# A hybrid diffusion step on one core: the prompt's convolution pool is made 2 KiB smaller, and the long convolution counts 0.55 of its cost when streams take turns

## The chip, the cores and the metric

The kernel runs on one core of a Trainium2 chip. The metric is the device time of one execution in microseconds (us). Engines are called by the profile's names: PE is TensorE (matmuls), PEld its weight loads, DVE is VectorE, ACT is ScalarE, POOL is GpSimd and SP is SyncE, which here issues nearly all DMAs.

## The reference

One trunk layer is computed for 2048 latent tokens and for 256 prompt tokens, D = 1024, in f32. Both groups go through the same head groups:

```
h = rms_norm(x) * (1 + scale1) + shift1;  u = h @ w_in            # 1024 -> 2560 columns
y_pool = pool_mixer(u[:256])          # windows 2/4/8/16 along the sequence, minus the token, 64x64 linear
y_hy   = hyena_mixer(u[256:1024])     # width-3 short convolution, then twice:
         # z = gate_o * (two_sided_fft_conv(z, k_o) + bias_o * z); k_o from a small sine MLP, decayed and normed
y_na   = attend(q, k, v)              # u[1024:2560]; latent: 2-D neighbourhood + 256 cached keys;
                                      # prompt: dense among its 256 tokens
x = x + gate1 * (concat(y_pool, y_hy, y_na) @ w_out)
x = x + gate2 * (relu(rms_norm(x) * (1 + scale2) + shift2 @ w_up)^2 @ w_down)
```

The outputs are both groups' x and the prompt's k and v. The long convolution of the latent tokens has length 2048 (FFT of 4096, done as matmuls with DFT matrices); the prompt's has length 256 (one dense DFT of 512).

## The kernel before, in words

**Three streams.** The program is written as three Python generators that `weave` takes turns among. Each `yield` names a cost. At every turn the stream with the least cost so far, divided by its weight, goes next; a stream that waits for a flag yields None and is passed over. The weights are 2200e3 for `dense`, 850e3 for `latent_mixers` and 700e3 for `prompt_mixers`. The turns fix the order in which instructions are written down. A list scheduler of the tile framework then gives each engine a fixed order at compile time: an instruction that was written earlier goes first when both are ready, and what `latent_mixers` and `prompt_mixers` write counts as 1000 and 2500 instructions earlier than its place. On the chip each engine works through its order and waits on semaphores.

**dense.** For each of five blocks of tokens (four of 512 latent tokens, number 4 is the prompt's 256) it computes the first 1024 columns of u (turns of 10 n each, eight per block, n the block's tokens), then, in the order 3, 4, 0, 1, 2, the q, k and v columns (`qkv_run`; 24 turns of 2600 for a latent block, 12 for the prompt's), then waits for the flag "prompt", then runs the output projection (`head`) and the MLP of the prompt, then of the latent blocks. All its matmuls write the PSUM tile `pm` and are made of three f32r products per f32 product (`mm3`, lines 126 to 128), for which each weight tile `wraw` is split into a high and a low part (ACT line 112, DVE line 115).

**latent_mixers.** It makes the filters of the long convolution (`filters`, with the second filter and the first transform only after the flags "u" and "ln"), then `hyena`: a spectrum product in pool `p2v` (16 steps, turns of 3 x 650), an inverse and forward transform in `p2w` (17 turns of 1300), a second spectrum product in `p2x`, and the last inverse transform in `p2y` (8 turns of 1550). Its matmuls write the PSUM tile `pf`. After the flags "qkv" and "prompt" it runs the latent attention (16 calls of `attend_latent`, each 230 + 8 x 1000 + 4 x 1800).

**prompt_mixers.** After the flags "h2p", "qkv4" (q, k and v of the prompt's block) and "ln" it makes the prompt's filters (pool `pfilt`, its result goes to the DRAM tile `Fpd`), then in pool `phy` the prompt's convolution (`prompt_hyena`, which begins with six `conv3`) and the pooling of both groups (`pooling`), then in pool `pat` the prompt's attention. Then it sets "prompt". Its matmuls write the PSUM tiles `pb` and `pbo`.

**Memory.** Pools without `side` are stacked from the low end of SBUF, those with `side="right"` from the high end. By the tile sizes, per partition: `p2v` and `p2x` hold bytes 107,872 to 161,120 (the last tile, the second `sg` buffer, starts at 159,072); `p2w` and `p2y` end at 159,072; `pfilt` begins at 169,696, `phy` at 159,200 (its first two tiles, `ppl`, lie at 159,200 to 161,248), `pat` at 175,712; all three end at 202,464, where `qkv` begins. A pool may take over bytes of a closed pool; the scheduler then makes its instructions wait for the old pool's.

Of the kernel before, what the change touches and what calls it, by code (L numbers as in the profile page):

```python
# [10 lines left out]
F32 = mybir.dt.float32  # L11
# [8 lines left out]
P = 128  # L20
# [35 lines left out]
def tile_hybrid_step(ctx: ExitStack, tc: tile.TileContext, a: dict):  # L56
# [20 lines left out]
    def pvs(name, i=0, n=1):  # L77
        o = PV[name][0] + i
        return pv[:, o:o + n]
# [26 lines left out]
    def split(pool, raw, shape, tag, lo_eng, bufs=None, n=None, hi_eng=None):  # L106
        hi = pool.tile(shape, F32R, tag=tag + "h", name=tag + "h", bufs=bufs)
        lo = pool.tile(shape, F32R, tag=tag + "l", name=tag + "l", bufs=bufs)
        if n is not None:
            hi, lo = hi[:, :n], lo[:, :n]  # L110
        if hi_eng is None:
            nc.scalar.activation(hi, raw, AF.Copy)  # L112
        else:
            hi_eng.tensor_scalar(out=hi, in0=raw, scalar1=1.0, scalar2=1.0, op0=ALU.mult, op1=ALU.mult)
        lo_eng.tensor_tensor(out=lo, in0=raw, in1=hi.bitcast(F32), op=ALU.subtract)  # L115
        return hi, lo
# [40 lines left out]
    def normed(pool, x, r, g, s, k, bufs, keep=False):  # L157

        n = x.shape[1]
        t = xp.tile([P, 512], F32, tag="raw", name="xn", bufs=3)[:, :n] if keep else x  # L160
        if k % 2:
            hi = pool.tile([P, 512], F32R, tag="hh", name="hh", bufs=bufs)[:, :n]
            lo = pool.tile([P, 512], F32R, tag="hl", name="hl", bufs=bufs)[:, :n]
            nc.vector.scalar_tensor_tensor(out=t, in0=x, scalar=g, in1=r, op0=ALU.mult, op1=ALU.mult)  # L164
            nc.scalar.activation(hi, t, AF.Identity, bias=s)
            nc.vector.scalar_tensor_tensor(out=lo, in0=t, scalar=s, in1=hi.bitcast(F32), op0=ALU.add, op1=ALU.subtract)  # L166
            return hi, lo
        nc.gpsimd.tensor_tensor(out=t, in0=x, in1=r, op=ALU.mult)
        nc.vector.tensor_scalar(out=t, in0=t, scalar1=g, scalar2=s, op0=ALU.mult, op1=ALU.add)  # L169
        return split(pool, t, [P, 512], "h", nc.gpsimd, n=n, bufs=bufs)  # L170

    def weave(*streams):


        live = [[st[0], float(st[1]), 0.0, st[2] if len(st) > 2 else 0] for st in streams]
        while live:
            for s in sorted(live, key=lambda e: e[2] / e[1]):
                try:
                    with tc.high_priority(s[3]) if s[3] else ExitStack():
                        cost = next(s[0])  # L180
                except StopIteration:
                    live.remove(s)
                    break
                if cost is not None:
                    s[2] += cost
                    yield cost
                    break
            else:
                yield None
# [10 lines left out]
    def wait_for(*names):  # L200
        while not done.issuperset(names):
            yield None

    def scope(name, bufs=2, side=None, **kw):
        return tc.tile_pool(name=name, bufs=bufs, side=side, reuse_waits="tile", **kw)
# [355 lines left out]
                fs1d.append((yield from filter_latent(o)))  # L561

    def conv3(hy, j, t0, L):
        u = hy.tile([P, L], F32, tag="cu", name="cu", bufs=2)
        nc.sync.dma_start(out=u, in_=uT[2 + j][:, t0:t0 + L])
        y = hy.tile([P, L], F32, tag="cy", name="cy", bufs=2)
        nc.scalar.activation(y, u, AF.Identity, scale=pvs("cw1", j), bias=pvs("cb", j))
        nc.vector.scalar_tensor_tensor(out=y[:, 1:L], in0=u[:, 0:L - 1], scalar=pvs("cw0", j), in1=y[:, 1:L], op0=ALU.mult, op1=ALU.add)
        nc.vector.scalar_tensor_tensor(out=y[:, 0:L - 1], in0=u[:, 1:L], scalar=pvs("cw2", j), in1=y[:, 0:L - 1], op0=ALU.mult, op1=ALU.add)
        return y  # L570
# [178 lines left out]
    def prompt_hyena(hy, bank):  # L749
        ppl = [[hy.tile([P, 2, P], F32, tag=f"ppl{j}{c}", name="ppl", bufs=1) for c in range(2)] for j in range(3)]  # L750
        for j in range(6):
            comp, half = j // 2, j % 2
            y = conv3(hy, j, NL, NP_)
            tr = bank()
            for e in range(2):
                nc.tensor.transpose(tr[:, e * P:(e + 1) * P], y[:, e * P:(e + 1) * P], ident)
            nc.scalar.activation(ppl[comp][half].rearrange("p e c -> p (e c)"), tr[:, :256], AF.Copy)
            yield 120
# [291 lines left out]
    def latent_mixers():  # L1050
        with scope("aps", 1, space=PSUM) as aps:
            turn = [0]

            def psum(tag=None):
                turn[0] ^= tag is None
                return aps.tile([P, 512], F32, tag=tag or "fz"[turn[0]], name="pf")

            yield from filters(psum)
            done.add("filt")
            yield from wait_for("u")  # L1060
            yield from wait_for("ln")
            with scope("hy") as kp:
                yield from hyena(kp, psum)
            done.add("hyena")
        yield from wait_for("qkv", "prompt")
        with scope("att") as at, scope("attps", 2, space=PSUM) as aps:
            def bank(tag):
                return aps.tile([P, 512], F32, tag=tag, name="p" + tag, bufs={"s": 2, "pt": 2, "o": 1}[tag])

            mask = []  # L1070
            for rc in range(3):
                for cc_ in range(3):
                    nr, ncol = ROWC[rc][1], COLC[cc_][1]
                    m = at.tile([P, nr, ncol], BF16, tag=f"mask{rc}{cc_}", name="mask", bufs=1)
                    nc.gpsimd.dma_start(out=m, in_=a["mask"][rc * 3 + cc_, :, 0:nr * ncol].rearrange("p (r c) -> p r c", c=ncol))
                    mask.append(m)
            for band in range(4):
                yield from wait_for(*(f"qkv{b}" for b in range(max(band - 1, 0), min(band + 2, 4))))
                for hp_ in range(4):
                    yield from attend_latent(at, bank, mask, band, hp_)  # L1080
                done.add(band)
        done.add("att")

    def head(rp, xpool, hpool, bank, which, n, c, src, rows, xs, hT):
# [29 lines left out]
        for k in range(KD):  # L1114
            hT.append(normed(hpool, xs[k], r, G2[:, k, c:c + 1], S2m[:, k, c:c + 1], k, bufs, keep=True))
# [40 lines left out]
    def qkv_run(qp, b, hT=None):  # L1156
        T0, n, c = run_of(b)
        if hT is None:
            r = qp.tile([P, 512], F32, tag="rq", name="rq", bufs=1)[:, :n]
            nc.sync.dma_start(out=r, in_=rsd[:, T0:T0 + n].broadcast_to([P, n]))  # L1160
            hT = []
            for k in range(KD):
                x = xp.tile([P, 512], F32, tag="raw", name="xq", bufs=3)[:, :n]
                nc.sync.dma_start(out=x, in_=xcols("xT_prompt", k, 0, n) if c else xcols("xT_sample", k, T0, n))
                hT.append(normed(hp, x, r, G1[:, k, c:c + 1], S1m[:, k, c:c + 1], k, 9))
        yield from proj_qkv(qp, hT, T0, n)
        done.add(f"qkv{b}")
# [98 lines left out]
    for cost in weave((dense(ctx.enter_context(ExitStack())), 2200e3), (latent_mixers(), 850e3, 1000), (prompt_mixers(), 700e3, 2500)):  # L1266
        assert cost is not None, "streams wait for each other"
# [177 lines left out]
def build(nc, arrays):  # L1445
    a = {}
    for name, v in arrays.items():
        a[name] = nc.dram_tensor(f"in_{name}", v.shape, mybir.dt.from_np(v.dtype), kind="ExternalInput").ap()
    for name, shape in _OUTS:
        a[name] = nc.dram_tensor(f"out_{name}", shape, F32, kind="ExternalOutput").ap()  # L1450
    with tile.TileContext(nc, schedule_with_timeline_sim=True) as tc:
        tile_hybrid_step(tc, a)
# [18 lines left out]
```

## Time and profile before

| | us |
|---|---|
| median of 3 runs (lowest, highest) | 3198.05 (3195.04, 3200.30) |
| the profiled execution, its own time | 3199.58 |
| its span in the profile | 3197.7 |
| PE busy in the span | 3044.0 (95%) |
| DVE, ACT, POOL busy | 1939.3 (61%), 1427.5 (45%), 958.1 (30%) |
| mean granted clock of PE, of full speed | 0.97 |

The span is the time from the first to the last instruction on the core; the profiled execution's own time is 1.9 us longer. Matmuls overlap in the records, so a busy PE need not be at its peak: how many matmuls a stretch holds (the number behind the x) tells more than its busy time.

### The profile page before, as it was taken

The numbers are of one execution on the slowest core, as the hardware profiler recorded it, in microseconds if no ns is written. First come the engines' busy times: TensorE is split into PE (matmuls) and PEld (weight loads), VectorE is DVE, ScalarE is ACT, GpSimd is POOL, SyncE is SP. The second block draws the span as 40 slices with busy tenths as digits, with TensorE's granted clock in tenths as the row PEclk, the third lists the DMA queues.
The fourth block names the chain that finished last, engine by engine and source line by source line (L and its number), as shares of the span: only waits on it lengthen the run. The fifth ranks groups of instructions, "written<-read, shape, count | busy, mean of one in ns | idle before, by whom it ended". The sixth has DMA issues, their size and how long they took to land.

```text
span 3197.7 us, 46181 instructions
## 1 busy us (share of the span) xinstructions
PE 3044.0 (95%) x16901; PEld 2512.5 (79%) x16901; DVE 1939.3 (61%) x3017; ACT 1427.5 (45%) x2721; POOL 958.1 (30%) x832
## 2 busy tenths in 40 slices
PE   5999999899898989999999999899999999999999
PEld 1667788799886879977887778688878888788887
DVE  7677676956777677878766545543564345644443
ACT  3555445545565566656555542332333223332222
POOL 2333233522543333446433321311231111311011
PEclk8999999999997899999999999899999999999999
DMA  6568667746973865553333335233324223332232
GB/s 223 161 211 296 218 208 235 250 149 215 291 240 113 273 194 176 181 183 101 121 118 109 104 110 176 79 93 102 115 92 145 95 97 113 98 119 99 92 99 86
DMA packets 255168, 494.26 MB, mean 155 GB/s; under 512 B 23763, under 2 KB 124824, under 8 KB 254619
## 3 DMA queue, kind: packets, MB, share of 16 engines
q1 hardware_dynamic: 247741, 469.03, 45.2%
q0 software_dynamic: 7200, 22.28, 2.5%
q8 instruction: 134, 2.20, 0.3%
q14 instruction: 93, 0.76, 0.1%
HBM read 421.86 MB, written 70.13 MB: 154 GB/s over the span
## 4 chain that ended last, share of the span: by engine, by line
PE 62%; DVE 2%; DMA 1%; ACT 1%; POOL 1%; issue 1%; SPq 0%; DVEq 0%; ACTq 0%; POOLq 0%
PE pm L126 18%; PE pm L128 18%; PE pm L127 18%; PE po L918 3%; PE ppt L897 2%; PE ps L883 1%; PE ps L884 1%; DVE xn L164 0%; DVE xn L169 0%; DVE wl L115 0%; DMA yraw<-yT 0%; DMA kin<-kT 0%; SPq L1009 0%; POOL ssq L150 0%; PE pm L154 0%
## 5 line engine op out<-in xcount | busy, mean ns | idle before, releaser
L115 DVE TENSOR_TENSOR wl<-wraw,wh 128x1024 fp32r<-128x1024 f32 x460 | 589.5, 1283 | 470.8 <-ACT wh L112 428.8
L112 ACT ACTIVATE wh<-wraw 128x1024 fp32r<-128x1024 f32 x430 | 454.6, 1058 | 781.1 <-PE pm L127 710.4
L126 PE MATMUL pm<-hh,wh 128*128 128x512 f32 (+1 forms) x1920 | 719.8, 377 | 19.6 <-ACT hh L112 11.4
L127 PE MATMUL pm<-hl,wh 128*128 128x512 f32 (+1 forms) x1920 | 718.2, 375 | 3.1 <-DVE hl L166 3.1
L128 PE MATMUL pm<-hh,wl 128*128 128x512 f32 (+1 forms) x1920 | 717.4, 374 | 0.0
L115 POOL TENSOR_TENSOR al<-r,ah 128x512 fp32r<-128x512 f32 (+1 forms) x160 | 199.5, 1248 | 967.0 <-ACT ah L112 966.8
L128 PE MATMUL pm<-ah,wl 128*128 128x512 f32 (+1 forms) x1280 | 475.7, 372 | 0.0
L127 PE MATMUL pm<-al,wh 128*128 128x512 f32 (+1 forms) x1280 | 473.3, 370 | 1.8 <-POOL al L115 1.8
L126 PE MATMUL pm<-ah,wh 128*128 128x512 f32 (+1 forms) x1280 | 473.2, 372 | 0.3 <-ACT wh L112 0.3
L126 PEld LDWEIGHTS pm<-hh,wh 128*128 128x128 f32 x1920 | 366.6, 191 | 101.0 <-issue 13.9
L127 PEld LDWEIGHTS pm<-hl,wh 128*128 128x128 f32 x1920 | 365.7, 190 | 74.5 <-issue 10.0
L128 PEld LDWEIGHTS pm<-hh,wl 128*128 128x128 f32 x1920 | 365.4, 190 | 70.0 <-issue 9.0
L1145 DVE SCALAR_TENSOR_TENSOR x<-pm,gate,x 128x512 f32<-128x512 f32 (+1 forms) x320 | 221.4, 695 | 274.1 <-PE pm L128 273.0
L127 PEld LDWEIGHTS pm<-al,wh 128*128 128x128 f32 x1280 | 240.9, 188 | 44.9 <-POOL al L115 2.0
L128 PEld LDWEIGHTS pm<-ah,wl 128*128 128x128 f32 x1280 | 240.9, 188 | 43.0 <-issue 1.7
L126 PEld LDWEIGHTS pm<-ah,wh 128*128 128x128 f32 x1280 | 240.6, 188 | 42.9 <-DVE x L1145 1.4
L127 PE MATMUL pm<-wl,hh 128*128 128x256 f32 x864 | 249.5, 291 | 5.3 <-DVE wl L115 5.3
L126 PE MATMUL pm<-wh,hh 128*128 128x256 f32 x864 | 247.6, 291 | 5.7 <-ACT hh L112 4.6
L128 PE MATMUL pm<-wh,hl 128*128 128x256 f32 x864 | 247.4, 291 | 3.9 <-POOL hl L115 3.1
L889 POOL TENSOR_SCALAR sS<-sS,rl 128x736 f32<-128x736 f32 (+5 forms) x128 | 126.7, 990 | 218.8 <-DVE rl L888 141.9
L127 PEld LDWEIGHTS pm<-wl,hh 128*128 128x128 f32 x864 | 167.2, 194 | 10.4 <-DVE wl L115 6.6
L126 PEld LDWEIGHTS pm<-wh,hh 128*128 128x128 f32 x864 | 166.5, 194 | 10.9 <-ACT hh L112 7.0
(325 smaller groups left out, 4841.1 us busy)
## 6 DMA issues: line engine op xcount, KB each, us to landing
wraw<-in_w_up SPq DMA_DIRECT2D x160, 512.0 KB
wraw<-in_w_down SPq DMA_DIRECT2D x160, 512.0 KB
wraw<-in_w_qkv SPq DMA_DIRECT2D x60, 512.0 KB
wraw<-in_w_u SPq DMA_DIRECT2D x40, 512.0 KB
dftw<-in_S POOLq DMA_DIRECT2D x40, 512.0 KB, 6.1
wraw<-in_w_out SPq DMA_DIRECT2D x40, 512.0 KB
x<-in_xT_sample SPq DMA_DIRECT2D x64, 256.0 KB
wm<-in_w_mod SPq DMA_DIRECT2D x64, 256.0 KB
```

The costliest lines, as they stand in the source:

```text
L112: nc.scalar.activation(hi, raw, AF.Copy)
L115: lo_eng.tensor_tensor(out=lo, in0=raw, in1=hi.bitcast(F32), op=ALU.subtract)
L126: nc.tensor.matmul(out, lh, rh, start=start, stop=False, **kw)
L127: nc.tensor.matmul(out, lh, rl, start=False, stop=False, **kw)
L128: nc.tensor.matmul(out, ll, rh, start=False, stop=stop, **kw)
L883: nc.tensor.matmul(out, qh[:, qc], krhs, start=True, stop=False, **kw)
L884: nc.tensor.matmul(out, ql[:, qc], krhs, start=False, stop=True, **kw)
L889: nc.gpsimd.tensor_scalar(out=sc_[:, :tot], in0=sc_[:, :tot], scalar1=r, scalar2=1.0, op0=ALU.mult, op1=ALU.mult)
L897: nc.tensor.transpose(tr[:n, q * P:(q + 1) * P], scs[e][:, so:so + n], ident)
L918: nc.tensor.matmul(po[64 * e:64 * e + 64, ocol:ocol + P], vap(e, n), pt[:n, col * P:(col + 1) * P], start=(q == 0), stop=(q == len(chunks) ...
L1145: nc.vector.scalar_tensor_tensor(out=xs[j], in0=po, scalar=gate2[:, j, c:c + 1], in1=xs[j], op0=ALU.mult, op1=ALU.add)
```

## The change

`conv3` gets one buffer instead of two for its input `cu` and for its output `cy` (four tiles of 1 KiB become two), so that `phy` holds 2 KiB less and begins at byte 161,248 instead of 159,200. And `hyena`'s turns are passed through `at_rate`, which multiplies each cost by 0.55 and passes None on, so that `weave` gives it 1/0.55 = 1.8 times as many turns for the same progress of the other streams. No instruction is added or removed; the order of all of them may move.

```diff
+    def at_rate(stream, f):
+
+        for cost in stream:
+            yield cost and cost * f
...
     def conv3(hy, j, t0, L):
-        u = hy.tile([P, L], F32, tag="cu", name="cu", bufs=2)
+        u = hy.tile([P, L], F32, tag="cu", name="cu", bufs=1)
         nc.sync.dma_start(out=u, in_=uT[2 + j][:, t0:t0 + L])
-        y = hy.tile([P, L], F32, tag="cy", name="cy", bufs=2)
+        y = hy.tile([P, L], F32, tag="cy", name="cy", bufs=1)
...
             with scope("hy") as kp:
-                yield from hyena(kp, psum)
+                yield from at_rate(hyena(kp, psum), 0.55)
             done.add("hyena")
```

## Rows read from the trace of the kernel before

**Rows 1.** The page, part 2: PE busy and granted clock, 40 slices of 80 us.
```profile
PE   5999999899898989999999999899999999999999
PEclk8999999999997899999999999899999999999999
```

**Rows 2.** Stages: PE, PEld, DVE, ACT, POOL busy (x instructions), PEclk, DMA share, GB/s.
```profile
526.00:640.00 114.00, 96.11 (x659) 84.12 (x659) 99.20 (x136) 59.92 (x114) 67.54 (x50) 0.91 0.79 256
640.00:764.00 124.00, 117.62 (x964) 115.46 (x964) 68.23 (x92) 51.97 (x98) 25.42 (x23) 1.00 0.46 145
764.00:893.00 129.00, 119.00 (x868) 113.91 (x867) 93.87 (x143) 70.84 (x145) 69.14 (x89) 0.96 0.91 296
893.00:947.00 54.00, 50.73 (x396) 48.74 (x395) 46.07 (x62) 34.43 (x71) 22.72 (x17) 0.97 0.76 238
947.00:1020.00 73.00, 55.76 (x259) 42.11 (x258) 54.53 (x88) 43.27 (x97) 35.98 (x29) 0.75 0.39 119
1020.00:1106.00 86.00, 77.07 (x560) 72.99 (x559) 64.14 (x88) 47.51 (x79) 23.82 (x28) 0.87 0.74 239
1106.00:1140.00 34.00, 22.70 (x173) 21.83 (x173) 19.36 (x31) 15.79 (x29) 13.18 (x17) 0.85 0.96 281
```

**Rows 3.** The same stages, instructions on `pm` alone: PE, PEld, DVE, ACT.
```profile
947.00:1020.00 73.00, 0.32 (x3) 0.12 (x1) 0.00 (x0) 0.00 (x0) 0.75 0.39 119
1020.00:1106.00 86.00, 51.72 (x396) 49.57 (x397) 11.36 (x24) 2.71 (x7) 0.87 0.74 239
1106.00:1140.00 34.00, 20.82 (x163) 20.33 (x163) 2.21 (x5) 1.49 (x4) 0.85 0.96 281
```

**Rows 4.** The tiles' first and last starts: prompt filters, conv3, spectrum, prompt attention.
```profile
L747 SPq DMA_DIRECT2D Fpd<-Fp x2: 326/367/408, 448.7 to 492.8; - x2
...
L565 SPq DMA_DIRECT2D cu<-uT x6: 319/420/667, 767.9 to 785.7; - x6
...
L661 ACT ACTIVATE sg<-pf x9: 577/581/602, 601.6 to 766.3; 128x512 f32<-128x512 f32 x9
...
L953 PE MATMUL pb<-ident,sS x32: 272/421/476, 934.7 to 1019.9; 128*128 128x128 f32 x32
```

**Rows 5.** Stages, instructions on `pf` alone.
```profile
526.00:640.00 114.00, 37.40 (x222) 32.07 (x222) 33.79 (x50) 14.20 (x24) 0.91 0.79 256
640.00:764.00 124.00, 9.54 (x60) 7.91 (x60) 10.59 (x16) 4.15 (x7) 1.00 0.46 145
...
947.00:1020.00 73.00, 36.61 (x180) 30.44 (x181) 28.37 (x42) 12.52 (x21) 0.75 0.39 119
1020.00:1106.00 86.00, 29.20 (x158) 24.78 (x158) 10.15 (x15) 10.88 (x20) 0.87 0.74 239
```

**Rows 6.** The stage 947 to 1020, instructions on `pb` alone.
```profile
947.00:1020.00 73.00, 12.82 (x52) 8.84 (x52) 4.15 (x6) 10.71 (x34) 0.75 0.39 119
```

**Rows 7.** The same stage, instructions on `pbo` alone.
```profile
947.00:1020.00 73.00, 9.83 (x24) 3.40 (x24) 0.00 (x0) 1.14 (x3) 0.75 0.39 119
```

**Rows 8.** What PE waited for from 1020 to 1140: total us, times, longest.
```profile
PE ps L883 <- ACT qh L991: 9.1, 1, 9.1
PE pf L126 <- ACT vsh L112: 3.1, 1, 3.1
PE pf L127 <- DVE vsl L115: 2.5, 2, 1.6
...
PE pf L703 <- DVE z L678: 1.7, 2, 0.9
```

**Rows 9.** DVE groups by shape, 526 to 640: busy, mean ns.
```profile
L115 DVE TENSOR_TENSOR ysl<-Y,ysh 128x512 fp32r<-128x512 f32 x12 | 10.5, 876 | 0.7 <-ACT ysh L112 0.6
...
L647 DVE TENSOR_TENSOR Y<-pf,F 64x512 f32<-64x512 f32 x13 | 8.8, 676 | 0.6 <-ACT F L641 0.5
```

**Rows 10.** A DVE group from 640 to 800.
```profile
L115 DVE TENSOR_TENSOR ysl<-Y,ysh 128x512 fp32r<-128x512 f32 x4 | 2.7, 685 | 0.3 <-ACT ysh L112 0.3
```

**Rows 11.** Latent attention: the first and last load, the first and last transpose.
```profile
L969 SPq DMA_DIRECT2D kin<-kT x16: 326/355/584, 1117.2 to 1732.0; - x16
...
L897 PE MATMUL ppt<-ident,sS x672: 270/273/421, 1142.4 to 1895.4; 128*128 128x128 f32 x96, 128*120 128x128 f32 x48, 128*96 128x128 f32 x8, 128*24 128x128 f32 x8
```

## The prediction

> **What bounds the kernel now.** I read the page's slices first: PE is the engine that is nearly always busy, and the reader is to see the thin spots, slices 12 to 14, where the granted clock also dips to 0.7 [rows 1]. The first slice and the single dips after slice 24 are a start and block changes that the diff does not touch. Then I cut the middle into stages by what each stream was doing [rows 2]. From 640 to 764 us PE took 964 matmuls in 124 us, one per 0.1286 us: that is dense work with little beside it, the full rate. From 764 to 893, with prompt work and the long convolution beside dense, it is one per 0.1486 us; from 526 to 640 one per 0.173. From 947 to 1020 only 259 matmuls ran in 73 us, with the granted clock at 0.75: part of that stage ran at 1.2 instead of 2.4 GHz, behind idle time on PE. By tile the reader sees why: in those 73 us dense started 3 matmuls, after which it started 396 in the next 86 [rows 3]. Dense had finished qkv and stood at "prompt", whose attention made its last transposes at 1019.9 [rows 4]; what ran was the second spectrum and the prompt's attention [rows 5 to 7]. So the stage is bounded by the prompt stream's end, and around it PE is starved.
>
> Why is the prompt that late? Its filters were stored at 492.8, its convolution's first load was issued at 767.9, and between them lies the end of the first spectrum, whose last `sg` was made at 766.3 [rows 4]. By the tile sizes `phy` takes bytes that `p2v`'s last `sg` buffer held (159,200 against 161,120), so I read these 275 us as a wait for memory. The spectrum itself was held back: 222 `pf` matmuls from 526 to 640, then 60 in the next 124 us [rows 5], while PE was full of dense work that had been written earlier.
>
> **The change, part by part.** Costs of turns: the u columns are 4 x 40960 + 20480 = 184,320; blocks 3 and 4 of qkv are 62,400 and 31,200. So dense stands at 277,920 / 2200e3 = 0.1263 when "qkv4" is set. The filters cost 70,800, so hyena begins at 70,800 / 850e3 = 0.0833 and has by then (0.1263 - 0.0833) x 850e3 = 36,600: before, `p2v` (31,200) was closed and `p2w` open, so `phy` could lie on `p2v`'s bytes. With 0.55 it has 66,500 real units, past `p2v` and `p2w` (53,300): `p2x` is open and ends at 161,120, and only the smaller `phy`, from 161,248, fits beside it. The two edits therefore go together.
>
> *conv3 with one buffer.* Nothing is computed less. The prompt's convolution no longer waits for `p2v`; what it still waits for is older (the second filter's transforms and the prompt's own filters, which end between 490 and 520). Its 256 us from 764 to 1020 [rows 2] then lie at some 520 to 780, or 60 us later if crowded; dense needs "prompt" at about 1008, so over 150 us of slack hide it. The price of one buffer: each of six loads waits on SP for the conv before it, and weight loads stand behind it on that queue. All six went out in 18 us [rows 4], some 3 us each. Bounds: nothing, as three `wraw` buffers and the slack cover it, and 18 us if each of six waits held a weight load that PE needed. I take nothing.
>
> *at_rate.* Hyena's 96,900 units count 53,300, so it is written out when dense stands at (70,800 + 53,300) / 850e3 = 0.146 instead of 0.197: 0.7 into the third qkv block instead of half into the fifth. The holding from 640 ends: 60 matmuls at the pace of 222 in 114 us need 31 of those 124 us, so 93 us are saved and hyena's chain, 526 to 1106, would end at about 1013. That is where qkv ends, as follows.
>
> *The sum.* Moved ahead of qkv's end: 180 + 158 `pf`, 52 `pb`, 24 `pbo`, together 414 matmuls [rows 5 to 7]. Their price is not shown; bounds 0.1286 (53 us) and 0.173 (72 us) each. I take 0.1486, the stage most like it (61.5 us): qkv ends at 947 + 61.5 = 1008.5. Then come the 396 + 163 `pm` matmuls that stood done at 1140 [rows 3]: 559 x 0.1286 = 71.9 us. From 1020 to 1140 there were 733 matmuls, 94.3 us of work in 120, so 25.7 us of pauses; 7.3 of them PE spent on hyena's `vsh`, `vsl` and `z` [rows 8], which are past. The others stay, 18.4 us: the norm inside the prompt's head, and the first attention matmul, for which PE stood 9.1 us. The state of 1140 is reached at 1008.5 + 71.9 + 18.4 = 1099, 41 us earlier. After that PE is full in nearly every slice [rows 1], so the gain is kept: 3199.6 (the profiled execution) - 41 = 3158.5. The median lies 1.5 below that execution: 3157.
>
> With the bounds: at 53 us and pauses cut to the 9.1, 947 + 53 + 72 + 9 = 1081, 59 us earlier (3139). At 72 us and all 25.7, 1117: 23 earlier (3175). The 18 us of conv3 on top would leave 5.
>
> **A row that speaks against it.** The work moves into stages where DVE is already 99.2 busy of 114 us [rows 2]. There the f32r split `ysl`, with both inputs in SBUF, took 876 ns [rows 9]; from 640 on, with POOL a third as busy, 685 [rows 10]. The product that reads one input from PSUM took 676 beside the same POOL work [rows 9]. The prompt's pooling brings more POOL work beside the spectrum, and so longer DVE instructions. The Trainium skill (SBUF — State Buffer, Who interferes with whom) says the same as a rule: DVE and GpSimd share a port pair under an exclusive lock, and a DVE instruction with two SBUF inputs waits a GpSimd one out. By that rule the crowded stretch would be paced by DVE and the time would be the third rival's; the trace agrees that such instructions stretch, and no run here shows yet whether PE then starves.
>
> **The rivals.**
>
> *More than forecast.* The pauses go too, and attention, which then starts with the prompt's head instead of 50 us into its MLP, fills its norm: the 59 us of the lower bounds, the last 9.1, and up to 12 of the 18 us in which PE stood from 526 to 640 [rows 2], if prompt work fills them: 59 to 80 us, 3130. For it: the prompt's head had no partner but hyena's last transforms. Against it: PE stood for attention's start itself [rows 8].
>
> *Attention's catch-up takes half.* When "qkv" is set, latent stands at 0.146 and dense at 0.2114, so (0.2114 - 0.146) x 850e3 / 15,430 = 3.6 attention calls are written before dense's next turn, against 0.8 before. A call took (1895.4 - 1117.2) / 16 = 48.6 us beside dense [rows 11]. If 2.8 calls run at double pace, 68 us, and PE has only 259/73 of 964/124 (0.46) to do, as from 947 to 1020, 37 us go; if dense fills in, nothing. The middle, 18: 3176. Against it: the list order lets ready dense matmuls through.
>
> *DVE paces the crowded stretch (slower).* DVE's work from 526 to 947 is 307 us, 54.5 come in from 947 to 1020 [rows 2], and some 35 of the next stage's 64 (an estimate by its 158 `pf` matmuls): 397 us in 482.5, 0.82 full. It was 0.87 full at most by stage, but 0.73 from 764 to 893, when the prompt ran [rows 2]. If dependences and POOL hold DVE to a fill f, qkv ends at 526 + 397 / f, and it decides against the change below 0.756, where that passes 1051 and the 41 us are gone. At 0.72 it ends at 1077: 27 us later than before, 3225.
>
> *It does not do what it says.* If another thing held the prompt (SP's order, PSUM banks), or the order puts it behind hyena, dense still stands at "prompt" near 1020: hyena merely leaves the stage 947 to 1020 emptier. 3198. Against it: filters and convolution stood 275 us apart with every input there.
>
> **How the numbers follow.** Forecast 0.54 (its own range 3139 to 3178), more 0.13, catch-up 0.13, no effect 0.09, DVE 0.11. The time is the likeliest case's, 3157. The range goes from 3118 (80 us, the upper end of the second case) to 3197: it leaves out the DVE case and part of the no-effect case. A measurement of this kernel tells 0.2%, 6.4 us, from no change. Faster: 0.54 + 0.13 + 0.13 = 0.80; same 0.09; slower 0.11.
>
> **What would show it.** Right: `cu` loads near 520; the prompt's last transposes before 850; no hold of `pf` from 640 to 764; dense's first `w_out` matmuls right behind its last qkv ones, at 1000 to 1015, and no stage of 70 us with 259 matmuls. Attention's first `kin` load then stands near 1015 instead of 1117.2. Wrong: qkv's end past 1040 with DVE over 0.8 busy all the way (third rival); `pm` matmuls thin after attention's start (catch-up); `cu` still behind `sg` (no effect). The likeliest error is the price of the 414 moved matmuls.

## The result: 32 us faster, and the profile after

| | before | after |
|---|---|---|
| median of 4 runs each, side by side (lowest, highest), us | 3196.55 (3192.04, 3200.30) | 3165.04 (3163.24, 3167.24) |
| ratio, 95% interval | | 0.9896 (0.9881, 0.9911) |
| span of the profiled execution, us | 3197.7 | 3161.5 |
| PE not busy in the span, us | 153.7 | 138.9 |
| mean granted clock | 0.970 | 0.978 |

The forecast was 3157, the time is 3165: the medians lie 31.5 us apart, where 41 was forecast, and the interval of the ratio is clear of 1. The thin slices 12 to 14 of [rows 1], counted from 0, have filled. Part 2 of the page after, PE busy and granted clock in 40 slices of 79 us:

```profile
PE   5999998889998999999999999899999999999999
PEclk8999999999999999999999999999999999999999
```

The reader sees what was bought and what was paid: slices 12 to 14, 8-9-8 with the clock at 7-8-9 before, are at 8-9-9 with the clock at 9, while slices 6 to 8, 9-8-9 before, are now at 8. The stages show the same. First PE, PEld, DVE, ACT, POOL (busy, instructions), granted clock, DMA share and GB/s, to be laid beside [rows 2]; then the instructions on `pf` alone, beside [rows 5]:

```profile
526.00:640.00 114.00, 94.26 (x567) 78.09 (x567) 105.57 (x154) 62.27 (x135) 83.99 (x83) 0.88 0.85 282
640.00:764.00 124.00, 113.01 (x849) 105.87 (x849) 95.37 (x143) 66.45 (x145) 50.22 (x45) 0.97 0.51 161
764.00:893.00 129.00, 119.87 (x937) 113.66 (x937) 68.97 (x93) 64.09 (x123) 37.32 (x40) 0.99 0.80 263
893.00:980.00 87.00, 84.78 (x700) 84.37 (x699) 72.42 (x101) 54.60 (x106) 38.33 (x29) 0.98 0.63 196
980.00:1060.00 80.00, 69.45 (x505) 65.73 (x504) 72.56 (x99) 47.05 (x82) 33.68 (x34) 0.87 0.66 226
1060.00:1094.00 34.00, 34.00 (x291) 34.00 (x290) 23.31 (x31) 21.00 (x33) 8.28 (x12) 1.00 0.89 284
1094.00:1140.00 46.00, 38.44 (x297) 37.16 (x296) 31.09 (x58) 24.48 (x49) 12.76 (x16) 0.89 0.83 266
```

```profile
526.00:640.00 114.00, 26.87 (x150) 22.20 (x151) 25.12 (x37) 9.45 (x16) 0.88 0.85 282
640.00:764.00 124.00, 21.11 (x126) 18.02 (x126) 16.51 (x25) 8.34 (x14) 0.97 0.51 161
764.00:893.00 129.00, 31.82 (x216) 27.88 (x216) 8.24 (x12) 10.73 (x18) 0.99 0.80 263
893.00:980.00 87.00, 25.35 (x174) 22.53 (x174) 27.94 (x41) 11.28 (x19) 0.98 0.63 196
```

Up to 764 us PE started 567 + 849 = 1416 matmuls against 659 + 964 = 1623 before, at a lower clock and with DVE 93% busy in the first stage. From 764 on it is fuller, and the stage of 73 us with 259 matmuls is gone. Hyena's own matmuls in the first stage fell (222 to 150): the prompt's work came between them.

The streams by tile, to be laid beside [rows 4] and [rows 11] (times of the first and last start at the end): the prompt's filters, its `conv3`, the 16 `sg` of the first spectrum, hyena's first transform load behind that spectrum, the prompt's last attention transposes, the latent attention's loads and transposes.

```profile
L752 SPq DMA_DIRECT2D Fpd<-Fp x2: 327/368/408, 445.4 to 489.5; - x2
...
L570 SPq DMA_DIRECT2D cu<-uT x6: 319/330/583, 520.0 to 564.5; - x6
...
L666 ACT ACTIVATE sg<-pf x16: 579/598/602, 558.4 to 776.5; 128x512 f32<-128x512 f32 x16
...
L673 SPq DMA_DIRECT2D V<-d1d x16: 360/377/623, 779.3 to 1070.7; - x16
...
L958 PE MATMUL pb<-ident,sS x32: 270/272/327, 709.4 to 809.2; 128*128 128x128 f32 x32
...
L974 SPq DMA_DIRECT2D kin<-kT x16: 319/336/471, 1107.7 to 1729.6; - x16
...
L902 PE MATMUL ppt<-ident,sS x672: 270/272/476, 1131.1 to 1880.8; 128*128 128x128 f32 x96, 128*120 128x128 f32 x48, 128*96 128x128 f32 x8, 128*24 128x128 f32 x8
```

The prompt is the part that moved: `cu` 248 us earlier, its last transposes 211 earlier. Hyena hardly did: the first spectrum's last `sg` is 10 us *later*, the latent attention's first transposes 11 earlier.

Dense itself tells where the gain stands. All kernels start 12,271 `pm` matmuls, and dense's parts end at the same numbers in the kernels before and after (within a part the order differs); counted in the records, the start of the n-th:

| dense matmul no. | what it is | before | after | change |
|---|---|---|---|---|
| 3657 | the last of qkv | 947.0 | 980.3 | +33 |
| 4214 | the state of 1140 us in the forecast | 1139.9 | 1093.8 | -46 |
| 5288 | about 1357 before | 1356.8 | 1308.9 | -48 |
| 7056 | attention is over | 1969.4 | 1933.7 | -36 |
| 12271 | the last | 3193.4 | 3157.1 | -36 |

Dense's place is not the whole state of PE, so the -46 and -48 flatter the change. At no. 4214 attention's start, which costs a pause, lies behind the kernel before and still ahead of the kernel after; and at no. 5288 the kernel after had started 154 attention matmuls fewer (`ps`, `ppt` and `po` by their records). The -36 behind attention is the gain.

What PE waited for from 1020 to 1140, the two longest, beside [rows 8]:

```profile
PE pm L126 <- ACT r L1132: 7.2, 1, 7.2
PE pf L127 <- DVE ysl L115: 3.0, 2, 2.2
```

The 9.1 us for attention's start did not go: they became the 7.2. The `r` of line 1132 is not the norm but the relu in the prompt's MLP (the norm's is line 135), and what ACT did just before it shows why it was late:

```profile
1111.80 2.41 ACT L877 ACTIVATE kst<-kin 64x704 fp32r<-64x704 f32 x3 [4.07 <-DMA kin<-kT]
1114.12 1.71 ACT L877 ACTIVATE ckst<-cin 64x256 fp32r<-64x256 f32 x4
1115.86 0.39 ACT L1132 ACTIVATE r<-pm 128x256 f32<-128x256 f32 x1
```

ACT works in its fixed order. Attention's first keys (`kst`, `ckst`) stood in it ahead of the relu; ACT waited 4.1 us for their load and worked 4.1 on them, and dense, which needs the relu, waited 7.2. In the kernel before, PE stood at attention's own first matmul for the same load.

### The profile page after: what moved, and what is told of

It is laid out like the page before. It is cut to its first block, busy times and chain, and to the rows that moved or that the text cites. A ratio compares the mean times of both kernels' runs of the same rounds, so it can differ in the third digit from the quotient of the medians.

```text
span 3161.5 us, 46164 instructions
## 1 busy us (share of the span) xinstructions
PE 3022.6 (96%) x16901; PEld 2494.6 (79%) x16901; DVE 1936.3 (61%) x3017; ACT 1428.6 (45%) x2721; POOL 951.3 (30%) x832
## 4 chain that ended last, share of the span: by engine, by line
PE 81%; DVE 8%; DMA 5%; issue 3%; ACT 2%; POOL 1%; SPq 1%; DVEq 0%; ACTq 0%; POOLq 0%
PE pm L126 22%; PE pm L127 22%; PE pm L128 22%; PE po L923 3%; PE ppt L902 2%; PE ps L888 1%; DVE wl L115 1%; PE ps L889 1%; PE pf L516 1%; PE pf L127 1%; DMA xq<-in_xT_sample 1%; PE pf L126 1%; PE pf L128 1%; PE pf L435 1%; DMA dftw<-in_S 1%
## 5 line engine op out<-in xcount | busy, mean ns | idle before, releaser
L126 PE MATMUL pm<-hh,wh 128*128 128x512 f32 (+1 forms) x1920 | 719.3, 377 | 22.7 <-ACT hh L112 12.8
```

The costliest lines, as they stand in the source:

```text
L126: nc.tensor.matmul(out, lh, rh, start=start, stop=False, **kw)
```

## The experiments

Twelve kernels ran. One table first, so that each group below can refer to it. "Prompt" is the start of the last `pb<-ident,sS` transpose, "spectrum" that of the first `V` load (the first spectrum is over), "hyena" that of the last `pf` matmul, "attention" that of the first `ppt` transpose. "Lost" is worked out from the view by stages, as the sum over nine stages from 526 to 2040 us (cut at 640, 764, 893, 985, 1092, 1200, 1330, 1480) of PE's not-busy time plus (1 - granted clock) x width, and given for 526 to 764 / 764 to 1200 / 1200 to 2040. For the stage 947 to 1020 of [rows 2], for instance, it is 17.2 + 18.3 = 35.5 of 73 us.

| kernel | time | ratio (95%) | prompt | spectrum | hyena | attention | lost |
|---|---|---|---|---|---|---|---|
| before | | 1 | 1019.9 | 778.0 | 1104.8 | 1142.4 | 35/93/40 |
| after | 3165.0 | 0.9896 (0.9881, 0.9911) | 809.2 | 779.3 | 1091.0 | 1131.1 | 48/49/28 |
| e1 pool alone | 3199.0 | 1.0002 (0.9993, 1.0012) | 811.6 | 837.4 | 1158.9 | 1200.1 | 51/68/44 |
| e2 0.70 alone | 3186.4 | 0.9961 (0.9946, 0.9975) | 993.1 | 747.9 | 1091.5 | 1132.2 | 38/76/38 |
| e3 both, 0.70 | 3190.1 | 0.9976 (0.9967, 0.9986) | 808.0 | 795.8 | 1114.6 | 1150.8 | 50/59/33 |
| e6 both, 0.60 | 3183.4 | 0.9943 (0.9922, 0.9963) | 810.1 | 792.1 | 1104.7 | 1147.5 | 49/62/32 |
| e5 both, 0.50 | 3169.6 | 0.9905 (0.9884, 0.9927) | 814.1 | 783.5 | 1100.5 | 1141.0 | 47/54/27 |
| e4 both, 0.40 | 3196.3 | 0.9995 (0.9985, 1.0005) | 810.4 | 763.2 | 1092.6 | 1136.0 | 52/73/40 |
| e7 pooling last | 3192.0 | 0.9974 (0.9964, 0.9984) | 753.7 | 772.9 | 1118.3 | 1157.2 | 47/68/31 |
| e8 latent lead 3000 | 3184.1 | 0.9947 (0.9928, 0.9967) | 813.2 | 707.3 | 1038.2 | 1074.4 | 58/63/37 |
| e9 0.55, first spectrum | 3165.1 | 0.9887 (0.9868, 0.9905) | 815.4 | 786.0 | 1101.4 | 1142.5 | 48/55/28 |
| e10 0.55, after it | 3207.7 | 1.0024 (1.0013, 1.0035) | 808.5 | 836.3 | 1159.2 | 1202.5 | 54/70/44 |
| e11 prompt lead 1500 | 3187.9 | 0.9956 (0.9941, 0.9971) | 813.3 | 706.0 | 1040.4 | 1076.9 | 58/67/33 |
| e12 pool, latent lead 1800 | 3186.8 | 0.9952 (0.9934, 0.997) | 815.7 | 712.4 | 1060.0 | 1094.5 | 60/65/33 |

The differences of the sums of "lost" to the kernel before go with those of the spans within 15 us (before to after: -42, the span -36), so to that accuracy the time of every kernel is PE's pauses and the slow clock around them. The times of events are those of one profiled execution, which can lie some us from the median (e9's took 3172.2, its median is 3165.1).

### The parts, each alone (e1, e2), and both at 0.70 (e3)

`e1_pool_only`: the smaller pool, no factor. `e2_rate_only_070`: the old pool with 0.70; by the tile sizes `phy` with two buffers (43,264 bytes) doesn't fit above `p2x` (41,344 left), so 0.55 alone was not tried. `e3_both_070`: both at 0.70.

```diff
-                yield from at_rate(hyena(kp, psum), 0.55)
+                yield from hyena(kp, psum)                   # e1
+                yield from at_rate(hyena(kp, psum), 0.70)    # e2 (cu, cy with bufs=2) and e3
```

> conv3 with one buffer, hyena at its full cost. Theory A, the gain comes from the prompt's stream ending before qkv does, wherever hyena stands: conv3's loads near 520 us, no stage in which dense waits for the prompt, and 0.985 to 0.993 of the kernel before, like the full change. Theory B, the share of hyena carries at least half: the long convolution is held behind dense and its end, with the start of the latent attention, moves past 1130 us (1106 and 1117 before), and the time is 0.994 to 1.0.

> conv3 with two buffers (phy lies on p2v's bytes), hyena's cost times 0.70, the least factor near 0.55 at which p2x is not yet open when phy is placed. Theory A: phy still waits for the first spectrum, so the prompt ends late and dense waits; hyena's spectrum is held less, so phy starts some 60 to 100 us earlier than 768 and part of the gain comes through that: 0.994 to 0.999. Theory B: 0.990 to 0.994, as most of the full change.

> Both parts, factor 0.70 instead of 0.55. Theory A: within 0.003 of the full change (0.987 to 0.993). Theory B: between the full change and the pool's part alone, nearer to the kernel before by a third of the share's part.

The pool alone frees the prompt (811.6) and gains nothing: theory A, by which the prompt's early end is the gain wherever hyena stands, falls in e1. B, by which hyena's share carries at least half, is right there, but not in size elsewhere: e2 came out at 0.9961, in A's range and above B's, and e3 at 0.9976, where B has some 0.993. The two effects don't add either: at 0.70 the pool's part is nothing that these intervals can tell (e2, e3). Where e1's gain goes is seen in dense: it ends qkv at 971.3, passes no. 4214 at 1098.4 and no. 5288 at 1303.1 (54 us ahead of before, more than after, but with the least attention work done), and no. 7056 at 1970.7, level with before. Stages of e1, all instructions, then `pm` alone:

```profile
1357.00:1391.00 34.00, 29.32 (x174) 20.64 (x173) 22.15 (x67) 22.44 (x69) 16.02 (x16) 0.76 0.40 114
...
1423.00:1441.00 18.00, 13.29 (x91) 9.49 (x91) 16.44 (x32) 12.82 (x33) 12.73 (x12) 0.86 0.37 104
```

```profile
1357.00:1391.00 34.00, 2.51 (x7) 1.26 (x5) 0.00 (x0) 0.00 (x0) 0.76 0.40 114
...
1423.00:1441.00 18.00, 2.08 (x4) 1.33 (x5) 0.00 (x0) 0.71 (x2) 0.86 0.37 104
```

Dense starts 7 matmuls in 34 us: it has done the prompt's head and MLP and stands at the head of the first latent block, which needs attention's output. It waited 31.2 us before no. 5475, and the load `yraw<-yT` of that output had gone out only at 1382.9. The 4 in 18 us are the norm inside that head, where the kernel after stands as well (16.8 us between two `pm` matmuls here, 14.9 there). Attention began 69 us later than in the kernel after, because hyena did: its first spectrum ended at 837.4 instead of 778.0. The same stage of the kernel after, `pm` alone:

```profile
1357.00:1391.00 34.00, 22.63 (x91) 16.31 (x90) 5.68 (x8) 0.00 (x0) 1.00 0.40 121
```

So the wait at "prompt" turned into a wait for the first latent block's attention, as long as hyena is late. e2 is the mirror: hyena's end is that of the kernel after, but the prompt is at 993.1, dense stands at "prompt" for 61 us, and about a third of the gain is there:

```profile
943.00:1004.00 61.00, 0.71 (x6) 0.52 (x6) 0.82 (x2) 0.00 (x0) 0.85 0.48 151
```

### Other factors (e4, e5, e6)

```diff
-                yield from at_rate(hyena(kp, psum), 0.55)
+                yield from at_rate(hyena(kp, psum), 0.40)    # e4; 0.50 in e5, 0.60 in e6
```

> Both parts, factor 0.40: hyena is written out earlier still, the second spectrum before the prompt's filters. Theory A, and hyena paced by the prompt's work and by DVE rather than by its place in the order: hyena ends within 15 us of the full change's 1092 and the time is within 0.003 of it. Theory B: hyena ends 30 us or more earlier, attention starts as much earlier, and the time is 0.983 to 0.988.

> Both parts, factor 0.50. The factors 1.0, 0.70, 0.55 and 0.40 gave 1.0002, 0.9976, 0.9896 and 0.9995. Theory C, smooth: the best factor lies near 0.5 between two costs (hyena late makes attention late; hyena early starves dense), so 0.50 gives 0.988 to 0.993. Theory D, each factor is another draw of the fixed order, whose stalls fall where they fall: anything from 0.988 to 1.0, with hyena's end within 20 us of 1092 all the same.

> Both parts, factor 0.60. Theory C: 0.990 to 0.994, between 0.55 and 0.70. Theory D: anything from 0.988 to 1.0; what tells is PE's idle time plus half its time at the low clock, which should account for the difference to the kernel before within 5 us in either case.

From 1.0 to 0.40 the ratios are 1.0002, 0.9976, 0.9943, 0.9896, 0.9905, 0.9995: a valley with its floor at 0.50 to 0.55, which speaks for theory C: the gain isn't one lucky order, as 0.50 has it too. But the valley is narrow, six points fit D's range as well, and D is not excluded. (e6's pauses and clock fell some 6 us more than its span, about the 5 expected of either theory.) Neither theory of e4 came out: hyena ended where A has it, but the time is not after's, and B's earlier end and gain are missing. At 0.40 the spectrum ended 16 us earlier than after, dense's qkv 23 later (1003.8), and hyena no earlier (1092.6): dense paid and nothing came back. Why hyena's later part then took 329 us instead of 312 was not found. Nor is it shown why the valley is so steep: e3's attention starts 8 us after e9's below (1150.8 against 1142.5), and its time is 25 us longer.

### Is it the crowd on DVE and POOL? (e7)

The pooling of both groups is taken out of the turns with the prompt's convolution and put behind the prompt's attention, in a pool of its own.

```diff
-                yield from weave((prompt_hyena(fp, bank), 14000), (pooling(fp, bank), 8100))
+                yield from prompt_hyena(fp, bank)
...
+            with scope("ppool", side="right") as fp:
+                yield from pooling(fp, bank)
```

> Both parts, factor 0.55, and the pooling (whose window sums run on GpSimd) behind the prompt's attention in a pool of its own instead of beside the prompt's convolution. Theory E, the first spectrum is paced by VectorE and GpSimd in the crowded stretch from 526 to 650: its f32r split falls from 1.1 us toward 0.88, qkv's end and hyena's end move 15 us or more earlier (987 and 1092 with the full change), time 0.982 to 0.987. Rival: the fixed order of PE holds hyena (46 us from 686 to 732 with the full change), hyena's end stays within 10 us of 1092 and the time within 0.003 of the full change's 0.9896.

DVE's splits with two SBUF inputs had indeed grown, from 876 ns [rows 9] to 1173 from 526 to 640, with POOL busy 84 of 114 us. The kernel after:

```profile
L115 DVE TENSOR_TENSOR ysl<-Y,ysh 128x512 fp32r<-128x512 f32 x8 | 9.4, 1173 | 0.7 <-ACT ysh L112 0.7
...
L652 DVE TENSOR_TENSOR Y<-pf,F 64x512 f32<-64x512 f32 x9 | 6.1, 676 | 0.5 <-ACT F L646 0.5
```

The product with a PSUM input stayed at 676. That agrees with the rule that the prediction cited (the Trainium skill, SBUF — State Buffer, Who interferes with whom). In e7 POOL falls to 49.7 us there and the split to 847 ns; two views of e7, the stage and the group:

```profile
526.00:640.00 114.00, 98.22 (x622) 84.05 (x621) 97.23 (x156) 56.74 (x114) 49.72 (x36) 0.90 0.83 271
```

```profile
L115 DVE TENSOR_TENSOR ysl<-Y,ysh 128x512 fp32r<-128x512 f32 x9 | 7.6, 847 | 2.0 <-ACT ysh L112 2.0
```

But what is lost up to 764 us is the same 47 against 48, the spectrum ends only 6 us earlier, and the time is 0.9974. So theory E falls as far as POOL goes: the longer DVE instructions are there, but with the split back at the length it had before (876) the spectrum is hardly earlier, and there is more loss from 764 to 1200 (68 against 49). DVE itself stayed 97.2 of 114 us busy, so whether its own work paces the spectrum is not decided. The rival missed too: the hold stayed, but hyena ended 27 us later (1118.3) and the time is 0.008 above after's. Why was not found.

### Which half of hyena needs the share (e9, e10)

`at_rate` gets bounds in cost units; the first spectrum is the first 31,200 of hyena's 96,900.

```diff
-    def at_rate(stream, f):
+    def at_rate(stream, f, lo, hi):
...
+        done = 0
         for cost in stream:
-            yield cost and cost * f
+            yield cost and cost * (f if lo <= done < hi else 1.0)
+            done += cost or 0
...
+                yield from at_rate(hyena(kp, psum), 0.55, 0, 31200)      # e9
+                yield from at_rate(hyena(kp, psum), 0.55, 31200, 1e9)    # e10
```

> The convolution pool is the smaller one, and the factor 0.55 holds only for the first spectrum's steps (31,200 of the long convolution's 96,900 cost units); from its transforms on each turn counts in full. So the whole stands for an even factor of (0.55 x 31,200 + 65,700) / 96,900 = 0.86. Theory F: only where the long convolution's end is written relative to dense counts, so the time lies on the line between the even factors 1.0 (1.0002 of the time before) and 0.70 (0.9976): 0.9985 to 0.9995. Theory G: the hold of the first spectrum behind dense work is what costs, so this half has at least half of the gain of the whole change: 0.991 to 0.995.

> The reverse: the first spectrum's turns count in full, the factor 0.55 holds from its transforms on (65,700 units). The whole stands for an even factor of (31,200 + 0.55 x 65,700) / 96,900 = 0.69. Theory F (the place of the written end): as the even factor 0.70, 0.996 to 0.998. Theory G (the first spectrum's hold): little of the gain is left, 0.998 to 1.001. If the crowd around the first spectrum were what the change loses, this would beat it: below 0.988, with the long convolution's end before 1090 us.

This is the clearest pair. The share on the first spectrum alone gives the whole gain (0.9887, with after's 0.9896 inside its interval); on the two thirds behind it, it gives nothing (1.0024, and the same late spectrum as e1). So theory F, by which only the written end counts, is wrong, and G holds, more strongly than it was put: the whole gain instead of half, and e10 a little above its range. e9 also sets the early prompt apart from hyena: its attention starts when that of the kernel before did (1142.5 against 1142.4), its prompt ends 204 us earlier, and the whole gain is there. First `V` loads of e9, then of e10:

```profile
L675 SPq DMA_DIRECT2D V<-d1d x16: 359/377/1050, 786.0 to 1081.1; - x16
```

```profile
L675 SPq DMA_DIRECT2D V<-d1d x16: 370/374/643, 836.3 to 1139.6; - x16
```

From its first `V` load to its last matmul hyena takes 312 to 348 us in all fourteen kernels, whatever its turns count there (e1 322, after 312, e10 323): that part isn't set by the share. What the share moves is the end of the first spectrum, which the early prompt had pushed from 778 to 837 and 0.55 pulls back to 779.

### Earlier still, by another way (e8, e11, e12)

`e8_latent_lead_3000`: the change, and what the latent stream writes counts as 3000 instead of 1000 instructions earlier. `e11_prompt_lead_1500`: the change, with the prompt's lead 1500 instead of 2500. `e12_pool_and_latent_lead_1800`: the pool, no factor, latent lead 1800.

```diff
-    ... (latent_mixers(), 850e3, 1000), (prompt_mixers(), 700e3, 2500)):
+    ... (latent_mixers(), 850e3, 3000), (prompt_mixers(), 700e3, 2500)):    # e8; 1800 in e12
+    ... (latent_mixers(), 850e3, 1000), (prompt_mixers(), 700e3, 1500)):    # e11
```

> Both parts, factor 0.55, and what the latent stream writes counts as 3000 instructions earlier than its place instead of 1000. If PE's holding of hyena comes from dense's place in the list, the hold from 686 to 732 goes, hyena ends 30 us or more before 1092 and attention starts as much earlier; time 0.980 to 0.988 if dense is not starved by it, 0.990 to 1.0 if it is. If the hold comes from when the scheduler thought hyena's inputs would be ready, nothing of hyena moves by more than 15 us.

> The whole change (0.55, smaller pool), but what the prompt's stream writes counts as 1500 instead of 2500 instructions earlier. In the changed kernel the prompt ended at 814 us and dense asked for it at about 985, 170 us later. Theory H: the prompt takes turns from the long convolution there that it doesn't need; with a smaller lead the prompt ends at 830 to 950 us, the long convolution 10 to 25 us before 1091, and the time is 0.983 to 0.988 of the time before. Theory I: the gain is a balance of all three streams, in which the long convolution's place counts against dense and the prompt's slack is filled work anyway: 0.989 to 0.996, and the long convolution's end stays within 8 us of 1091.

> The smaller pool, no factor on the long convolution, but what the latent stream writes counts as 1800 instead of 1000 instructions earlier. With the pool alone the time was that of before (1.0002): the wait went from the prompt's end to the first attention work, which began at 1187 us. Theory F': it is the latent stream's place in the list against dense that the factor sets, so a lead can replace it: the attention's first matmul before 1150 us and 0.990 to 0.996. Rival: the share in the turns does something that a lead doesn't (it moves the turns of the other two streams too): 0.998 to 1.002.

All three pull the spectrum's end to 706 to 712 us and attention's start to 1074 to 1095, and all three lie at 0.995. The hold of the spectrum thus comes from its place in the list: with enough lead it goes (from 686 to 732 us 52 `pf` matmuls in e8, 6 in the kernel after). A lead can stand for the share in part (F' in e12), but more of it isn't better. In e11 both theories missed: hyena came 51 us earlier, not 10 to 25 (H) or none (I), the prompt's end stayed at 813, and the time was in I's range for another reason. A stage of e11, all instructions, then `pm` alone, and the same of the kernel after:

```profile
1012.00:1078.00 66.00, 37.70 (x248) 34.17 (x247) 37.11 (x64) 29.11 (x54) 21.57 (x29) 0.74 0.80 254
```

```profile
1012.00:1078.00 66.00, 23.08 (x162) 21.27 (x161) 7.58 (x16) 0.84 (x2) 0.74 0.80 254
```

```profile
1012.00:1078.00 66.00, 59.81 (x454) 57.20 (x453) 55.80 (x75) 41.81 (x70) 23.33 (x28) 0.90 0.78 274
```

By the way of counting above, e11 loses 45.5 us in this stage and the kernel after 12.8; the difference is as large as that of their whole sums (158.5 against 125.2). One wait makes most of it. PE's longest from 1012 to 1085, and what ACT and POOL did before it ended:

```profile
PE pm L154 <- POOL ssq L150: 19.6, 1, 19.6
```

```profile
1061.67 2.42 ACT L877 ACTIVATE kst<-kin 64x704 fp32r<-64x704 f32 x3 [9.24 <-DMA kin<-kT]
1063.99 1.72 ACT L877 ACTIVATE ckst<-cin 64x256 fp32r<-64x256 f32 x4
1065.73 0.42 ACT L149 ACTIVATE sqr<-x 128x256 f32<-128x256 f32 x1
```

```profile
1065.65 0.89 POOL L1025 TENSOR_TENSOR Tt<-bias,mask 128x264 f32<-128x264 f32 x1 [9.63 <-DMA bias<-in_biasw]
1066.50 0.90 POOL L150 TENSOR_TENSOR ssq<-ssq,sqr 128x256 f32<-128x256 f32 x1
```

It is attention's start again. Its first keys and bias stand in the orders of ACT and POOL ahead of the last square (`sqr`) and sum (`ssq`) of the norm in the prompt's head. Both engines wait some 9 us for attention's loads, dense waits for the norm, hyena has ended, and no other matmul runs. e8 has the same wait with 19.1 us; in the other twelve kernels PE's longest wait within some 10 us of attention's first `kst` is 4.8 to 11.1 us. So what stands behind attention's first loads in the fixed orders decides what its start costs. e12 doesn't have the long wait (8.7 us), and its time of 0.995 is not accounted for by it.

## Why the prediction was right, and where its steps were not

- **The wait at "prompt" is a wait for memory**: right. `cu` went out at 520, the prompt's transposes ended at 809, and the pool alone (e1) does that.
- **Price of one buffer for `conv3`**: the six loads took 44.5 us instead of 18, 26 more, and as dense asked for "prompt" only at 980, it cost nothing.
- **at_rate ends the hold, and hyena ends at 1013**: wrong; this is the step that failed. The spectrum was crowded by the prompt (150 `pf` matmuls instead of 222 up to 640) and still held after (126 up to 764); it ended at 779, where it was before, and hyena at 1091; the sign that went with it, attention's first `kin` load near 1015, came at 1107.7. The prediction took the two edits as two gains. The runs showed that the first edit costs the first spectrum 59 us (837.4 against 778.0) and the second gives 58 back.
- **414 matmuls move ahead of qkv's end for 61.5 us**: too many, too cheap. By the stages 3053 were started from 526 to 980, against 2887 from 526 to 947 [rows 2]: 166, of which 108 are `pf`, for 33 us, 0.20 us each and above the upper bound of 0.173. The term came out at +33 where +61.5 was forecast.
- **From qkv's end to the state of 1140 us**: forecast 71.9 + 18.4 = 90.3 us, measured 980.3 to 1093.8, 113.5, since 230 `pf` matmuls that were taken as past still ran there. The state came at 1093.8 instead of 1099, but without attention's start, whose 9.1 us the forecast had put into the 18.4 and which came right behind (7.2 us, and 10.2 us at half the clock from 1111.4, another 5.1). With it the state is at about 1106, 34 us earlier instead of 41.
- **The total**: 41 us forecast, some 34 measured at that state, out of two terms that were far off: qkv ended 28 us sooner than forecast, and what follows took some 35 us longer. That the errors oppose each other has a reason, since hyena's work that didn't move ahead of qkv's end had to be done behind it; that they cancel to 7 us is luck.
- **The gain is kept**: right. 36 us are left at the end, and from 1200 to 2040 us the kernel after lost 28 us against 40. The second rival, attention's catch-up (18 us given back while attention runs), has no sign here.
- **DVE paces the crowded stretch**: DVE was busy 342.3 of 454 us from 526 to 980 (the first four stages), a fill of 0.754, at the value (0.756) where this rival was to decide. It didn't decide, since DVE's work in the stretch was 342 us, not 397: hyena had moved less. From 526 to 764 the loss rose from 35 to 48 us; that DVE's crowd is the cause is not shown (e7).
- **No effect, or the whole of the pauses**: the first is ruled out for the whole change, but it is what the pool alone gives (1.0002), by another mechanism than the one named: not that the prompt stays late, but that hyena becomes late. Of the second, attention's start kept its pause, 7.2 us instead of 9.1.

What is shown: the early prompt isn't enough (e1, e10), and the share is needed only in the first spectrum (e9). That the early prompt is needed for the whole gain rests on e2 and e9: hyena as early as after without it gives 0.9961, attention as late as before with it 0.9887. It is not shown at one factor, since 0.55 doesn't fit without the smaller pool and at 0.70 the pool adds nothing. What is open: why the gain falls off so steeply on both sides of 0.50 to 0.55, why 0.40 and e7 slow hyena's later part, and where e12 loses what its lead should have gained.

## What to carry to other kernels

When three streams fill one engine, a stream that is freed early takes its time from the one beside it; ask which stream's end is waited for next, and compare all streams' ends, not only the one that the edit frees. A lead or share had an optimum with losses on both sides here: too late and the wait stood at the next consumer (e1), too early and the next stream's first loads held ACT and POOL in front of the main stream's norm (e8, e11). Counting where the n-th matmul of the main stream stands in both traces shows in one table where a gain is made, but count the other streams' matmuls at the same points too: a main stream that is ahead may only have left more of the others undone. And before a wait is named by its tile, look the line up: `r` was a relu, and the cause stood two instructions earlier on ACT.

## What the hardware showed that was not expected

A pause on PE came with slow clock of about its own size where pauses are dense: in the stage 947 to 1020 before, 17.2 us not busy came with 18.3 us of clock [rows 2], part of that stage being granted 1.2 instead of 2.4 GHz behind the idle time. In e11, 1050 to 1078 us, the granted clock was 0.51, behind the wait of 19.6 us. Over the whole span before it was less, 153.7 and 95.9 us. The change took away 14.8 us of PE's pauses (153.7 to 138.9) and 26.3 of clock, (1 - 0.970) x 3197.7 = 95.9 against (1 - 0.978) x 3161.5 = 69.6: together 41 us, and the span fell by 36.2. And a DVE split with two SBUF inputs grew from 685 [rows 10] to 1173 ns with POOL at 84 of 114 us; with POOL at 50 of 114 us it took 847, and that bought no time (e7).
